# A 256-token trunk with a gated delta rule: the inverses' small transfers move from SyncE's queue to GpSimd's, and the scatter back is cut into four

## The chip, the cores and the metric

One core of a Trainium2 chip runs the whole kernel: a two-layer trunk for 256 tokens of width 2048, in float32. The metric is the device time of one execution in microseconds (us); lower is better. Every weight is read from HBM once per execution, 437 MB in all.

The engines are named as the profile names them: PE (TensorE's matmuls) and PEld (its weight loads), DVE (VectorE), ACT (ScalarE), POOL (GpSimd), and SP (SyncE). SP computes nothing here: it issues transfers in program order, and what stands behind a transfer that waits stands still too. SPq in a row of the profile is SP's queue.

## The reference, cut to what matters

The change lies in the first layer's mixer, a gated delta rule with 16 heads of width 128:

```python
kb = k * beta[..., None]
lower = jnp.where(strict, jnp.einsum('bnhid,bnhjd->bnhij', kb, k) * decay, 0.0)
rhs = jnp.concatenate([v * beta[..., None], kb * jnp.exp(g)[..., None]], axis=-1)
sol = lax.linalg.triangular_solve(lower, rhs, left_side=True, lower=True, unit_diagonal=True)
```

For every head a unit lower triangular system is solved, whose matrix comes from the products of the head's keys with each other. Nothing can be solved before the keys of that head exist, and no head's output can be had before its system is solved. Around it stand the projections k, q, z, v (`gdn_w_in`) and the output projection, and after it a feed-forward layer, an attention layer and a second feed-forward layer.

## The kernel before, in words

**The weight stream.** All projections go through `half` (L188): one piece of weights, 128 x 1024 float32 (512 KB), is loaded by SP into one of four `raw` tiles (L185), ACT rounds it to float32r (`hi`, L206), DVE forms the rest (`lo` = raw - hi, L207), and PE multiplies both by the 256 tokens (L228, L229: eight pairs of matmuls per piece). `raw`, `hi` and `lo` have four tiles each, so SP can load only some pieces ahead of PE. Each of z's and v's 16 heads takes two pieces.

**Things due later.** `after_halves(n, fn)` (L178) emits `fn` at the (n+1)th call of `half` from there on, just before that piece's load. In the order that SP executes, transfers therefore stand between two pieces of weights. SP's order is the written order; the other engines' orders come from a scheduler.

**The delta rule's inverses.** The order of the projections is k and q by heads, then z by heads, then v by heads.
- `products` (L552) makes a head's products of keys and writes them over the decays in `ma1` (first 128 tokens) and `ma2` (the other 128); DVE's L568 to L571 finish them. The sums of squares of keys and queries (`ssk`, `ssq`) come with them.
- `units_out` (L666) writes the 32 x 32 diagonal blocks of four heads to a DRAM scratch `um`: two tiles by four blocks, eight transfers (L675). It is emitted 11 pieces (`UM_LAG`) after each fourth head's products.
- `scales` (L506) writes the factors `cc`, transposed to `cT`, to the scratch `uc` with two transfers (L508), 11 pieces after the last products.
- `eliminate` (L677) is emitted two pieces later. It loads `um` and `uc` back with one block to a partition (L682, L684), and POOL inverts 128 blocks at once: L688, then 31 steps of a product (L692) and a subtraction (L695), then a transposing copy (L696). POOL also computes two inverse square roots (L174, L175) for `rq` and `rbt` around there.
- `there` (L698) writes the result to scratch in both layouts, `ut` and `un` (L699, L700), 31 pieces (`BACK_AT`) after the last products; `back` (L702), two pieces later, scatters it into the two tiles `T128` with 14 transfers (L707, L710).
- `merge` (L714), emitted at the 18th of the z and v projections, i.e. after all of z and the first of v, builds the 128-token inverses on PE from 32 x 32 matmuls (`iw`, L732; `ix`, L737) and 64 x 64 ones (`iy`).

All of these transfers are issued by SP, among the loads of weights.

Of the kernel before, what the change touches and what calls it, by code (L numbers as in the profile page):

```python
# [32 lines left out]
UM_LAG, BACK_AT, MERGE_AT = 11, 31, 17  # L33
# [21 lines left out]
class Lazy:  # L55
    """Tiles that are taken when they are first used."""
# [10 lines left out]
class Split:  # L67
    """A transposed activation [P, nk, 256] as two float32r parts, four k to a tile."""
# [22 lines left out]
class Trunk:  # L91
# [78 lines left out]
    def rsqrt(self, dst, src, scale):  # L170
        """dst = (src * scale + EPS) ** -0.5, exactly rounded powers, [P, n]."""
        nc = self.nc
        n = dst.free_size()
        nc.gpsimd.tensor_scalar(dst, src, scale, EPS, op0=ALU.mult, op1=ALU.add)  # L174
        nc.gpsimd.tensor_tensor(dst, dst, self.nhalf[:, :n], op=ALU.pow)  # L175

# [1 line left out]
    def after_halves(self, n, fn):  # L178
        """Emit fn once n more pieces of weights are under way."""
        self.due.append([n, fn])  # L180
# [7 lines left out]
    def half(self, src, name, apart=False):  # L188
        """One [P, 1024] piece of weights as two float32r parts that add up to it exactly."""
        nc = self.nc  # L190
        for d in self.due:
            d[0] -= 1
            if d[0] < 0:
                d[1]()
        self.due = [d for d in self.due if d[0] >= 0]
        cut = 2 if self.ahead else 1
        raw = self.ahead.pop(0) if self.ahead else self.raw(src, name)
        if apart:
            x = self.q(f"held_{name}", F32R)
            hi, lo = x[:, 0:1024], x[:, 1024:2048]  # L200
        else:
            hi = self.stp.tile([P, 1024], F32R, tag="hi", bufs=HI, name=f"hi_{name}")
            lo = self.stp.tile([P, 1024], F32R, tag="lo", bufs=LO, name=f"lo_{name}")
        for i in range(cut):
            c = slice(i * 1024 // cut, (i + 1) * 1024 // cut)
            nc.scalar.copy(hi[:, c], raw[:, c])  # L206
            nc.vector.tensor_tensor(lo[:, c], raw[:, c], hi[:, c].bitcast(F32), op=ALU.subtract)  # L207
        return hi, lo

    def wstat(self, srcs, xT, name, early=0):  # L210
        """For each source of weights, [P channels, 512]: columns 0:256 hold hi*hi, 256:512 the
        cross terms, for 256 tokens. Of the first `early` k the first 128 tokens go ahead."""
# [19 lines left out]
    def wstats(self, srcs, xT, first, name):  # L232
        """wstat over many sources, the first few side by side."""
# [5 lines left out]
    def add_halves(self, dst, ps, name, rows=slice(0, P), scaled=True):  # L239
        """The two halves' sum, for every token times its norm's factor."""  # L240
# [7 lines left out]
    def xstat(self, src, nk, xT, evac, name, ahead=0):  # L248
        """[tokens, 2048] = xT.T @ weights, a block of 512 columns at a time. In the last `ahead`
        pieces the first 128 tokens go ahead of the others."""  # L250
# [36 lines left out]
    def square(self, tt, q):  # L287
        """A part of the sum of h^2 over a token's row."""
        junk = self.t([P, 512], "jk", "junk", dtype=BF16)
        self.nc.scalar.activation(junk, self.h[:, tt, q * 512:(q + 1) * 512], AF.Square, accum_out=self.ssh[:, tt, q:q + 1])  # L290
# [8 lines left out]
    def pair(self, name):  # L299
        """Two banks, for even and odd k, so that two engines can read them at once."""  # L300
        return [self.ax(f"{name}_{i}") for i in range(2)]

    def enter_first(self):
        """What the first 128 tokens let begin: half of the first EARLY k of xT."""
# [19 lines left out]
    def enter(self):  # L324
        """xT = (h * weight).T in two parts, and every token's factor rsqrt(mean(h^2) + eps):
        self.r [tokens, 1] twice, self.rb the same along the columns of every partition."""
# [69 lines left out]
    def begin_post(self, which, name):  # L396
        """Room for a sublayer's result, and its norm's weights on every partition."""
# [24 lines left out]
    def update(self, tt, c, n):  # L422
        """h += result * factor, for n columns from c on."""
# [5 lines left out]
    def gdn(self):  # L429
# [12 lines left out]
        # the tensor engine's clock rises while it is kept busy  # L442
# [24 lines left out]
        # per token and head: c = beta / |k|^2, rb = beta / |k|, rq = scale / |q|  # L467
        g = {n: self.cst.tile([P, 2, NH], F32, name=n) for n in ("ssk", "ssq", "cc", "negc", "rbt", "rq")}
        dram = lambda n, shape: self.scr.tile(shape, F32, name=n)  # noqa: E731
# [4 lines left out]
        def multiply(h, kq):  # L474
            self.products(h, kq, MA1, MA2, g)
            if h % 4 == 3:
                self.after_halves(UM_LAG, lambda: self.units_out(h // 4, ma1, ma2))
# [28 lines left out]
        def scales():  # L506
            for p in range(2):
                nc.sync.dma_start(  # L508
# [3 lines left out]
        def eliminate():  # L512
            self.back = self.eliminate(cT, T128, units)
            fl = lambda x: x.rearrange("p a h -> p (a h)")  # noqa: E731
# [4 lines left out]

        self.after_halves(UM_LAG, scales)  # L520
        self.after_halves(UM_LAG + 2, eliminate)
        self.after_halves(BACK_AT, lambda: self.back[0]())
        self.after_halves(BACK_AT + 2, lambda: self.back[1]())
# [28 lines left out]
    def products(self, h, kq, MA1, MA2, g):  # L552
        """The masked and decayed products of a head's keys with its keys and queries."""
# [30 lines left out]
    def gates_and_decays(self, ps, ma1, ma2, szt):  # L584
# [3 lines left out]
        # room of z's tiles: after[s, j] = s > j, upto[s, i] = s <= i, and what is needed on the way  # L588
# [27 lines left out]
        # log1p(e) = e * ln(1 + e) / ((1 + e) - 1), and e where 1 + e rounds to 1  # L616
# [16 lines left out]
        # decay[j, i] = exp(sum of g over j < s <= i)  # L633
        sfx = self.t([P, NH], "sfx", "sfx", bufs=1)
        for q in range(4):
# [15 lines left out]
            v = lambda x: x.rearrange("p (h i) -> p h i", h=4)  # noqa: E731  # L651
# [12 lines left out]
    # The inverses of I + c M: on blocks of 32 tokens by elimination with one block to a partition,  # L664
    # unit = (p, b, h), then block by block on the tensor engine.
    def units_out(self, grp, ma1, ma2):  # L666
        """Four heads' diagonal blocks to their units' rows."""
        for p, ms in ((0, ma1), (1, ma2)):
# [3 lines left out]
            for b in range(4):  # L672
                bs = slice(b * 32, (b + 1) * 32)
                u = (p * 4 + b) * NH + grp * 4
                self.nc.sync.dma_start(self.um[u:u + 4].rearrange("h j i -> j h i"), m[bs, h0:h0 + 4, 0, bs])  # L675

    def eliminate(self, cT, T128, room):  # L677
# [4 lines left out]
        nc.sync.dma_start(m, um)  # L682
        cu = self.t([P, 32], "uc", "uc", bufs=1)
        nc.sync.dma_start(cu, uc)  # L684
# [13 lines left out]
        def there():  # L698
            nc.sync.dma_start(ut, m)  # L699
            nc.sync.dma_start(un, tu)  # L700

        def back():  # L702
            for p in range(2):
                for b in range(4):
                    u = slice((p * 4 + b) * NH, (p * 4 + b + 1) * NH)
# [6 lines left out]
        return there, back  # L712

    def merge(self, ma1, ma2, cc, T128, room):  # L714
        """T128[p][c, h, i]: the transposed inverses on 128 tokens. Its blocks' inverses as they
        are lie in [0:64, :, 64:128] and [64:96, :, 0:32] until they have been used."""
# [41 lines left out]
    def head(self, h, vT, MA1, MA2, T128, negc, rb, rq):  # L758
# [15 lines left out]
        # the heads' outputs, tokens on partitions  # L774
# [85 lines left out]
    def weights_of(self, h, kq, aT):  # L860
        """aT[key, (q0 k0 | q1 k0 | q1 k1)]: the transposed difference of the two softmaxes."""
# [155 lines left out]
```

## Time and profile before

| | |
|---|---|
| time, median of 3 runs | 2448.48 us (2447.5 to 2450.08) |
| profiled execution: its own time, the span from first to last instruction | 2455.4 us |
| PE busy | 2421.8 us, 99% |
| PEld busy | 2070.3 us, 84% |
| DVE busy | 1666.7 us, 68% |
| ACT busy | 1197.6 us, 49% |
| POOL busy | 116.7 us, 5% |
| mean granted TensorE clock | 0.993 of full speed |

The profiled execution is one run with the hardware profiler on; nothing of its time is given beside the span. Shares are means over the whole span. The stage in question, the first mixer with its output projection, takes about the first 510 us; z's and v's projections and the delta rule stand in it from about 230 us on.

A row of a timeline gives the start in us from the beginning of the span, the duration, engine, line, operation, out<-in, and a count where several were merged; in brackets stands how long the engine was idle before it, and who ended that.

### The profile page before, as it was taken

What the parts mean: (1) busy time and instruction counts of PE and PEld (TensorE: products, weight loads), DVE (VectorE), ACT (ScalarE), POOL (GpSimd) and SP (SyncE); (2) the same over time, 40 slices, a digit from 0 to 9 for tenths busy, and PEclk for the clock granted to TensorE, in tenths of its full rate; (3) what the DMA queues carried; (4) which work ended last, traced back from release to release, by engine and by line L of the source; (5) the groups of instructions that cost most, each with busy time, mean ns of one, the idle gap of its engine ahead of it and who ended that gap; (6) DMA issues with size and microseconds to landing.
All of it is one profiled execution on the core that took longest, in us unless ns stands there. A gap on an engine that the chain in (4) does not pass through costs nothing.

```text
span 2455.4 us, 35164 instructions
## 1 busy us (share of the span) xinstructions
PE 2421.8 (99%) x13267; PEld 2070.3 (84%) x13267; DVE 1666.7 (68%) x2603; ACT 1197.6 (49%) x1958; POOL 116.7 (5%) x185
## 2 busy tenths in 40 slices
PE   9999979999999999999999999999999999999998
PEld 7788869878888888888888888888888888888887
DVE  6888647857777777764446677555877777774444
ACT  6755424546444444443446555444644444444442
POOL 0100730100000000000000000000000000000000
PEclk9999989999999999999999999999999999999999
DMA  6365543444555555565554554555555555556554
GB/s 224 105 200 167 194 141 121 163 163 162 190 188 187 185 187 188 184 206 194 194 192 146 198 183 162 170 189 189 169 192 189 189 189 190 192 189 210 191 196 153
DMA packets 134731, 443.21 MB, mean 181 GB/s; under 512 B 26144, under 2 KB 26400, under 8 KB 134048
## 3 DMA queue, kind: packets, MB, share of 16 engines
q1 hardware_dynamic: 134560, 440.95, 54.4%
q8 instruction: 104, 1.70, 0.3%
q14 instruction: 67, 0.55, 0.1%
HBM read 437.21 MB, written 3.69 MB: 180 GB/s over the span
## 4 chain that ended last, share of the span: by engine, by line
PE 93%; POOL 2%; DVE 1%; ACT 1%; DMA 1%; SPq 1%; issue 1%; DVEq 0%; POOLq 0%; ACTq 0%
PE ps_up L228 26%; PE ps_up L229 13%; PE ps_d L283 7%; PE ps_d L284 7%; PE ps_d L282 6%; PE ps_v L228 3%; PE ps_ak L228 2%; PE ps_aq L228 2%; PE ps_k L228 2%; PE ps_q L228 2%; PE ps_v L229 1%; PE ps_wo L283 1%; PE ps_av L282 1%; PE ps_av L284 1%; PE ps_av L283 1%; PE ps_ao L284 1%
## 5 line engine op out<-in xcount | busy, mean ns | idle before, releaser
L228 PE MATMUL ps_up<-xT_f,hi_up 128*128 128x512 f32 x2752 | 964.1, 396 | 0.0
L229 PE MATMUL ps_up<-xT_f,lo_up 128*128 128x256 f32 x2752 | 767.5, 279 | 1.6 <-DVE lo_up L207 1.6
L228 PEld LDWEIGHTS ps_up<-xT_f,hi_up 128*128 128x128 f32 x2752 | 516.4, 188 | 123.6
L206 ACT CAST hi_up<-raw_up 128x1024 fp32r<-128x1024 f32 x344 | 361.1, 1051 | 482.1 <-issue 328.9
L207 DVE TENSOR_TENSOR lo_up<-raw_up,hi_up 128x1024 fp32r<-128x1024 f32 x344 | 421.1, 1225 | 202.4 <-ACT hi_up L206 202.1
L229 PEld LDWEIGHTS ps_up<-xT_f,lo_up 128*128 128x128 f32 x2752 | 518.3, 188 | 3.0 <-DVE lo_up L207 2.7
L207 DVE TENSOR_TENSOR lo_d<-raw_d,hi_d 128x1024 fp32r<-128x1024 f32 x168 | 205.8, 1225 | 224.2 <-ACT hi_d L206 224.2
L206 ACT CAST hi_d<-raw_d 128x1024 fp32r<-128x1024 f32 x168 | 177.1, 1054 | 256.5 <-PE ps_d L284 239.6
L282 PE MATMUL ps_d<-hi_d,hT 128*128 128x512 f32 x672 | 261.5, 389 | 0.0
L284 PE MATMUL ps_d<-hi_d,hT 128*128 128x512 f32 x672 | 261.4, 389 | 0.0
L283 PE MATMUL ps_d<-lo_d,hT 128*128 128x512 f32 x672 | 261.4, 389 | 0.0
L282 PEld LDWEIGHTS ps_d<-hi_d,hT 128*128 128x128 f32 x672 | 126.2, 188 | 26.2
L284 PEld LDWEIGHTS ps_d<-hi_d,hT 128*128 128x128 f32 x672 | 126.2, 188 | 26.2
L283 PEld LDWEIGHTS ps_d<-lo_d,hT 128*128 128x128 f32 x672 | 126.2, 188 | 26.1
L228 PE MATMUL ps_z<-xT_in,hi_z 128*128 128x512 f32 x256 | 92.4, 404 | 9.8 <-ACT hi_z L206 9.8
L228 PE MATMUL ps_v<-xT_in,hi_v 128*128 128x512 f32 x256 | 97.8, 417 | 2.3 <-ACT hi_v L206 2.3
L228 PE MATMUL ps_k<-xT_in,hi_k 128*128 128x512 f32 x240 | 88.3, 406 | 0.8 <-DVE s L244 0.8
L228 PE MATMUL ps_ak<-xT_kv,hi_ak 128*128 128x512 f32 x240 | 86.9, 402 | 0.0
L813 DVE SCALAR_TENSOR_TENSOR gy<-gs,c_fconv,gy 128x255 f32<-128x255 f32 (+1 forms) x176 | 84.5, 480 | 2.8
L228 PE MATMUL ps_q<-xT_in,hi_q 128*128 128x512 f32 x240 | 85.5, 397 | 0.3 <-DVE s L244 0.3
L228 PE MATMUL ps_aq<-xT_q,hi_aq 128*128 128x512 f32 x224 | 78.2, 392 | 0.0
L174 POOL TENSOR_SCALAR qr<-q 128x1 f32<-128x1 f32 x8 | 1.5, 193 | 1588.0 <-DVE q L409 1588.0
(382 smaller groups left out, 4122.9 us busy)
## 6 DMA issues: line engine op xcount, KB each, us to landing
raw_up<-in_w_up SPq DMA_DIRECT2D x344, 512.0 KB, 4.2
raw_d<-in_w_dn SPq DMA_DIRECT2D x176, 512.0 KB, 3.5
raw_z<-in_w_in SPq DMA_DIRECT2D x32, 512.0 KB, 3.6
raw_v<-in_w_in SPq DMA_DIRECT2D x32, 512.0 KB, 3.5
raw_wo<-in_w_out SPq DMA_DIRECT2D x32, 512.0 KB, 4.1
raw_av<-in_w_v SPq DMA_DIRECT2D x32, 512.0 KB, 3.4
raw_ao<-in_w_o SPq DMA_DIRECT2D x32, 512.0 KB, 3.5
raw_k<-in_w_in SPq DMA_DIRECT2D x30, 512.0 KB, 3.5
```

What stands on the lines that cost most here:

```text
L174: nc.gpsimd.tensor_scalar(dst, src, scale, EPS, op0=ALU.mult, op1=ALU.add)
L206: nc.scalar.copy(hi[:, c], raw[:, c])
L207: nc.vector.tensor_tensor(lo[:, c], raw[:, c], hi[:, c].bitcast(F32), op=ALU.subtract)
L228: nc.tensor.matmul(to, hi[:, w], x, start=(k == 0 and tt != 1), stop=False)
L229: nc.tensor.matmul(lt, lo[:, w], lx, start=False, stop=(k == KD - 1))
L282: nc.tensor.matmul(ps, xh, hi[:, w], start=(k == 0), stop=False)
L283: nc.tensor.matmul(ps, xh, lo[:, w], start=False, stop=False)
L284: nc.tensor.matmul(ps, xl, hi[:, w], start=False, stop=(k == nk - 1))
L813: nc.vector.scalar_tensor_tensor(y[:, j:S], s[:, 0:S - j], w[:, l, f, 2 - j:3 - j], y[:, j:S], op0=ALU.mult, op1=ALU.add)
```

## The change

The lines of the changed kernel have the same numbers up to L697 and numbers higher by one from the scatter on (L708 for L707, L733 for L732); comments that fell away are left out of the diff.

```diff
-UM_LAG, BACK_AT, MERGE_AT = 11, 31, 17
+BACK_AT, MERGE_AT = 30, 17
...
         def multiply(h, kq):
             self.products(h, kq, MA1, MA2, g)
             if h % 4 == 3:
-                self.after_halves(UM_LAG, lambda: self.units_out(h // 4, ma1, ma2))
+                self.units_out(h // 4, ma1, ma2)
...
         def scales():
             for p in range(2):
-                nc.sync.dma_start(
+                nc.gpsimd.dma_start(
                     self.uc[p * 64:(p + 1) * 64].rearrange("(b h) i -> h b i", b=4),
                     cT[p * NH:(p + 1) * NH].rearrange("h (b i) -> h b i", b=4))
...
-        self.after_halves(UM_LAG, scales)
-        self.after_halves(UM_LAG + 2, eliminate)
-        self.after_halves(BACK_AT, lambda: self.back[0]())
-        self.after_halves(BACK_AT + 2, lambda: self.back[1]())
+        scales()
+        eliminate()
+        for i in range(4):
+            self.after_halves(BACK_AT + i, lambda i=i: self.back(i))
...
-                self.nc.sync.dma_start(self.um[u:u + 4].rearrange("h j i -> j h i"), m[bs, h0:h0 + 4, 0, bs])
+                self.nc.gpsimd.dma_start(self.um[u:u + 4].rearrange("h j i -> j h i"), m[bs, h0:h0 + 4, 0, bs])
...
-        nc.sync.dma_start(m, um)
+        nc.gpsimd.dma_start(m, um)
         cu = self.t([P, 32], "uc", "uc", bufs=1)
-        nc.sync.dma_start(cu, uc)
+        nc.gpsimd.dma_start(cu, uc)
...
-        def there():
-            nc.sync.dma_start(ut, m)
-            nc.sync.dma_start(un, tu)
-
-        def back():
+        nc.gpsimd.dma_start(ut, m)
+        nc.gpsimd.dma_start(un, tu)
+
+        def back(i):
             for p in range(2):
                 for b in range(4):
+                    if b != i:
+                        continue
...
-        return there, back
+        return back
```

The 38 transfers of `um`, `uc`, `units`, `ut` and `un` are now issued by POOL, at the place in the program where their data are made; the 14 of the scatter stay with SP, in four parts (one for each block of 32 tokens: four, four, four and two transfers) ahead of four pieces in a row, from one piece earlier than `there` stood.

The first place is POOL's order where the last four heads' blocks go out and the elimination begins (`ma` tiles hold the products, `um_d` and `uc_d` are the scratch, `units` the elimination's tile). Before:

```order
L687 MEMSET units 128x32
L174 TENSOR_SCALAR rq<-ssq 128x32
L175 TENSOR_TENSOR rq<-rq,nhalf 128x32
L174 TENSOR_SCALAR rbt<-ssk 128x32
L518 TENSOR_SCALAR rq<-rq 128x32
L175 TENSOR_TENSOR rbt<-rbt,nhalf 128x32
L516 TENSOR_TENSOR rbt<-rbt,bgT 128x32
L688 TENSOR_TENSOR units<-units,uc 128x1024
```

And with the change, the last heads' transfers alone:

```order
L675 DMA um_d<-ma_3_388 32x4x32 x4
L174 TENSOR_SCALAR rq<-ssq 128x32
L175 TENSOR_TENSOR rq<-rq,nhalf 128x32
L174 TENSOR_SCALAR rbt<-ssk 128x32
L675 DMA um_d<-ma_1_390 32x4x32 x4
L518 TENSOR_SCALAR rq<-rq 128x32
L175 TENSOR_TENSOR rbt<-rbt,nhalf 128x32
L508 DMA uc_d<-cT 16x4x32 x2
L682 DMA units<-um_d 128x1024
L516 TENSOR_TENSOR rbt<-rbt,bgT 128x32
L684 DMA uc<-uc_d 128x32
L688 TENSOR_TENSOR units<-units,uc 128x1024
```

Ahead of and among the same six small operations now stand twelve transfers, eight of them behind the first power (L175), and L688 comes last.

The second place is SP's order around the scatter. Before (`t_0` and `t_1` are the two `T128` tiles):

```order
L185 DMA raw_z_0_1_3403<-in_w_in 128x1024
L185 DMA raw_z_0_0_3432<-in_w_in 128x1024
L699 DMA ut_d<-units 128x1024
L700 DMA un_d<-units 128x1024
L185 DMA raw_z_0_1_3456<-in_w_in 128x1024
L185 DMA raw_v_0_0_3485<-in_w_in 128x1024
L707 DMA t_0_2541<-ut_d 32x16x32
```

With the change:

```order
L185 DMA raw_z_0_1_3405<-in_w_in 128x1024
L708 DMA t_0_2549<-ut_d 32x16x32
L711 DMA t_0_2549<-un_d 32x16x32
L708 DMA t_1_2550<-ut_d 32x16x32
L711 DMA t_1_2550<-un_d 32x16x32
L185 DMA raw_z_0_0_3438<-in_w_in 128x1024
L708 DMA t_0_2549<-ut_d 32x16x32
L711 DMA t_0_2549<-un_d 32x16x32
L708 DMA t_1_2550<-ut_d 32x16x32
L711 DMA t_1_2550<-un_d 32x16x32
L185 DMA raw_z_0_1_3464<-in_w_in 128x1024
```

The first transfer that needs the elimination now stands ahead of both pieces of z's last head, where before it stood between them, and it is a read of `ut`, where before it was the write of `ut`. On PE the first 16 of `merge`'s `iw` matmuls now stand ahead of z's last head, where before the first `iw` stood between the two pieces of v's first head.

## Rows read from the trace of the kernel before

**Rows 1.** The page's first part: span, and busy time by engine.

```profile
span 2455.4 us, 35164 instructions
PE 2421.8 (99%) x13267; PEld 2070.3 (84%) x13267; DVE 1666.7 (68%) x2603; ACT 1197.6 (49%) x1958; POOL 116.7 (5%) x185
```

**Rows 2.** PE's timeline around z's last head and v's first.

```profile
334.99 0.80 PE L228 MATMUL ps_z<-xT_in,hi_z 128*128 128x512 f32 x1 [9.80 <-ACT hi_z L206]
...
340.56 0.40 PE L228 MATMUL ps_v<-xT_in,hi_v 128*128 128x512 f32 x1
...
343.43 0.62 PE L732 MATMUL iw<-t,ma 32*32 32x32 f32 x14
346.36 0.51 PE L228 MATMUL ps_v<-xT_in,hi_v 128*128 128x512 f32 x1 [2.31 <-ACT hi_v L206]
...
352.68 1.54 PE L732 MATMUL iw<-t,ma 32*32 32x32 f32 x36
354.15 0.50 PE L228 MATMUL ps_v<-xT_in,hi_v 128*128 128x512 f32 x1
```

**Rows 3.** Stretches of 2 us: length, busy by engine (PE, PEld, DVE, ACT, POOL), granted clock, DMA.

```profile
332.00:334.00 2.00, 0.00 (x0) 0.00 (x0) 0.00 (x0) 0.11 (x1) 0.00 (x0) 0.50 0.88 314
...
350.00:352.00 2.00, 2.00 (x8) 1.71 (x8) 1.71 (x2) 0.80 (x1) 0.00 (x0) 0.50 0.77 227
```

**Rows 4.** Waits of SP's queue, 300 to 360 us: total, times, longest.

```profile
SPq L699 <- POOL units L696: 21.4, 1, 21.4
```

**Rows 5.** The chain of waits, 318 to 362 us: start, us, what.

```profile
327.42 4.13 DMA un_d<-units
...
331.93 0.49 SPq L707
332.46 0.49 SPq L710
...
341.23 4.01 DMA raw_v<-in_w_in
```

**Rows 6.** POOL's timeline, from the decays' last operation to the elimination's end.

```profile
99.03 0.15 POOL L687 MEMSET units<- 128x32 f32 x1
253.28 0.68 POOL L174 TENSOR_SCALAR rq<-ssq 128x32 f32<-128x32 f32 x1 [154.10 <-ACT jq L564]
254.04 5.45 POOL L175 TENSOR_TENSOR rq<-rq,nhalf 128x32 f32<-128x32 f32 x1
...
265.78 0.96 POOL L516 TENSOR_TENSOR rbt<-rbt,bgT 128x32 f32<-128x32 f32 x1
268.22 2.40 POOL L688 TENSOR_TENSOR units<-units,uc 128x1024 f32<-128x1024 f32 x1 [1.49 <-DMA uc<-uc_d]
270.70 0.30 POOL L692 TENSOR_TENSOR pr<-units 128x31 f32<-128x31 f32 x1
271.08 1.14 POOL L695 TENSOR_TENSOR units<-units,pr 128x31 f32<-128x31 f32 x1
...
325.11 1.91 POOL L696 COPY units<-units 128x1024 f32<-128x1024 f32 x1
```

**Rows 7.** POOL in two stretches with the same 16 shapes: length, busy, clock, DMA.

```profile
270.70:285.56 14.86, 13.64 (x16) 1.00 0.72 246
317.30:325.04 7.74, 6.56 (x16) 1.00 0.00 0
```

**Rows 8.** DVE's timeline: the last heads' products, and its last operation before the idle stretch.

```profile
248.53 0.42 DVE L569 TENSOR_TENSOR ma<-p,ma 128x256 f32<-128x256 f32 x1
...
317.66 0.43 DVE L246 TENSOR_TENSOR zs<-zs,rb_in 128x256 f32<-128x256 f32 x1
```

**Rows 9.** DMA issues: out<-in, queue, count, KB each, median us to landing.

```profile
um_d<-ma SPq DMA_DIRECT2D x32, 16.0 KB, 2.0
units<-um_d SPq DMA_DIRECT2D x1, 512.0 KB, 5.8
ut_d<-units SPq DMA_DIRECT2D x1, 512.0 KB, 2.6
```

**Rows 10.** z's weights (raw_z), 290 to 345 us: seven loads.

```profile
DMA to landing us min/median/max: 3.4/3.4/5.9
```

## The prediction

> **What bounds the kernel now.** The page comes first: of a span of 2455.4 us PE is busy 2421.8 us [rows 1]. The stream of weights through PE is the bound; a change counts only where it makes or closes a hole in PE, or where PE runs slower. PE's timeline shows the holes that belong to this change [rows 2]. Ahead of the second piece of z's last head PE is idle for 9.80 us (until 334.99), ahead of the second piece of v's first head for 2.31 us. The short stretches show what follows a hole [rows 3]: the granted clock is 0.50, the lower of the two levels (1.2 GHz), in the idle stretch around 333 us and again at 350 to 352 us, where PE is busy. So the piece that starts at 334.99 lasts until 340.56, 5.57 us, while the next, at full clock, takes 2.87 (340.56 to 343.43) [rows 2].
>
> The hole's cause is found in SP's waits: it stood 21.4 us at L699 until POOL's copy L696 was done [rows 4], and every load of weights behind stood with it. Then the two results are written (the second lands 4.13 us after its issue), the scatter goes out at 0.53 us a transfer (331.93 to 332.46), and only at 341.23 the next load [rows 5]. So the start of POOL's elimination and its length decide. POOL idles 154.10 us until the last query's sum of squares, runs the small operations from 253.28 to 266.74, waits 1.49 us for data and starts L688 at 268.22; the copy ends at 327.02 [rows 6].
>
> One property of the elimination matters below. Its shapes run up from 31 to 256 columns and down again, so its first 16 and last 16 operations are the same work: 14.86 us while DVE works, 7.74 us in the last stretch [rows 7], nearly all of it after DVE's last operation at 317.66 [rows 8]. Beside a working DVE it is 1.92 times slower.
>
> **The change, part by part.** I compare when PE starts the third piece of v (354.15 before [rows 2]); all holes of the change lie ahead of it, and behind it the work is the same.
>
> *Early transfers.* The first three groups of four heads (24 transfers) move to POOL's idle 154 us and off SP's queue, where PE had no hole: nothing gained. If that cover were gone, they would delay the elimination by their issue time.
>
> *Price of an issue on POOL, d.* No row of before shows a transfer issued by POOL. Nearest below: SP's 0.49 us for a scatter transfer [rows 5]. Nearest above: 2.0 us, as if POOL stood until `um` has landed [rows 9]. A reason excludes a gain: on POOL the issues stand in series with the elimination. I take SP's 0.49 plus the 0.84 by which POOL's same-sized operations differ beside a busy DVE (1.14 against 0.30 [rows 6]): d = 1.33.
>
> *The start.* The fourth group's first four transfers are ready at 248.95 [rows 8] and end at 248.95 + 4d = 254.27, 0.99 later than 253.28, where the power chain began. From its start to the start of its last operation (253.28 to 265.78 [rows 6]) are 12.5 us, and four more `um`, two `uc_d` and the `units` load now stand in between: 7d = 9.31. So the load is issued by 276.1. It landed 5.8 us after its issue began [rows 9], 5.5 after it ended: L688 starts at about 281.5, not 268.22, **13.3 us later**. The `uc` load, issued 0.96 + d later and small, I let land with it.
>
> *The elimination.* What slides by 13.3 us was run beside DVE and now falls after 317.66, where DVE has nothing to do because its weights are held up: 13.3 / 1.92 = 6.9. It ends at 327.02 + 6.9 = 333.9.
>
> *The way back.* POOL issues both writes (2d = 2.7), and SP's first scatter transfer waits for the landing, by 2.3 (2.6 less SP's issue [rows 9]) to 3.7 (4.13 less it [rows 5]): 3.0. SP is free at 339.6; before, its waits were over at 331.6. Queued behind it are both pieces of z's last head.
>
> *Restart.* Four scatter transfers at 0.53 (2.12), then the load: 4.01 [rows 5] to 5.9 [rows 10], I take 5.0; ACT's cast to PE's start 1.12 (345.24 to 346.36, [rows 2, 5]). That is 8.24. One piece at the low clock 5.57, three at 2.87, and the second half of the tile's `iw` (32 of 64 records at 1.54 / 36 each, 1.4) [rows 2]; the first half hides in the hole. Together 23.8, and the scatter (some 2.7 us a piece on SP) keeps ahead of PE. The 2.31 us hole and the second slow stretch of before are gone in this sum: that is the gain of the four parts. PE starts v's third piece at 339.6 + 23.8 = 363.4, not 354.15: **+9.3 us**.
>
> Bounds: d = 0.49 with the fast landings starts L688 6.4 us later and gives +2.3; d = 0 gives about nothing. d = 2.0 with slow landings starts it 20.6 later and gives +16.
>
> The profiled execution took 2455.4 us, 0.3% above the median of 2448.48; I put the sum on the median unscaled: 2457.8.
>
> On the lock between POOL and DVE: the row shows 14.86 against 7.74 us. The Trainium skill (SBUF — State Buffer, "SBUF: two separate sides") says that a DVE operation with two SBUF inputs and a POOL operation that reads SBUF shut each other out for whole instructions, and that a transfer issued by POOL can't write its descriptors while DVE holds the ports in its two-port modes. This speaks against the change; by it each issue could wait out one of DVE's operations, and the sum would come to about +12 (an estimate from that page's rule, with 1.2 us for such a DVE operation).
>
> **The rivals.**
>
> *1. Cheap issue: no change.* POOL only hands a transfer over, d below 0.65. L688 then starts 3 to 8 us later and the sum lies between 0 and +4.9, 2451 at its middle. For it: SP's bare issue is 0.49. Against it: POOL does its own operations between and slows beside DVE, which SP does not. The Trainium skill (DMA: Bandwidth & Descriptors, "Anatomy of one DMA") calls descriptor generation small and puts most of a POOL transfer's fixed time after the issue; no row here shows it.
>
> *2. The elimination meets DVE less: faster.* Which operations collide depends on when they start. If from 281.5 on none did, the middle part would take 46.6 / 1.92 = 24.3 us (270.70 to 317.30 before [rows 6, 7]) and the rest 7.74; with L688, the copy and the gaps it ends at 318.0, SP is free at 323.7, and v's third piece starts at 347.5: -6.6, so 2441.8. It decides once SP is free before 330.3, that is, once the elimination ends by 324.6. Against it: DVE runs the same operations at the same pace as long as weights flow, so the collisions should be as many.
>
> *3. POOL stands longer than a landing, d above 2.* Beyond 1.33 each 0.1 us of d costs about 0.8 us (seven and four issues through the 1.92, and two on the way back), so d = 2.5 gives +18: 2466.5. For it: eight issues stand in a row on the critical engine.
>
> That the transfers do not leave earlier where it matters is part of the forecast: the fourth group left SP as soon as DVE was done, and now half of it stands behind a power of 5.45 us [rows 6].
>
> **How the numbers follow.** Forecast (d from 0.65 to 2, +5 to +16): 0.65. Rival 1: 0.19. Rival 2: 0.06. Rival 3: 0.10. A measurement of this kernel can tell about 0.2% (4.9 us) from no change. So faster 0.06, same 0.19, slower 0.65 + 0.10 = 0.75. The range reaches down into rival 1, to +1 (2449.5), and up past the upper bound into rival 3, +18.5 (2467); the likeliest case alone is 2453.5 to 2464.5.
>
> **What would show it.** POOL's L688 starts near 281 us (275 if d is small); the copy L696 ends near 334; SP's longest wait is at its first scatter transfer (L708) and lasts over 30 us; PE's hole ahead of z's last head runs from about 322 us, one piece (2.87) earlier than before, to about 348, some 25 us; the 2.31 us hole in v's first head is gone. I am wrong if L688 starts before 272 us, if the elimination is shorter than 46 us, or if PE's hole there stays under 13 us.

## The result, and the profile after

| | before | after |
|---|---|---|
| median | 2448.8 us (7 runs, 2445.61 to 2456.68) | 2459.58 us (7 runs, 2452.94 to 2467.58) |
| ratio, 95% interval | 1 | 1.0051 [1.0036, 1.0065] |
| profiled execution, span | 2455.4 us | 2464.6 us |
| z's first matmul | 235.90 us | 234.91 us |
| L688 starts / the copy L696 ends | 268.22 / 327.02 | 275.00 / 328.94 |
| v's third piece starts | 354.15 us | 357.20 us |
| w_out's first matmul starts / its last ends | 477.04 / 577.17 | 481.45 / 586.07 |

The changed kernel is slower, by about 12 us going by the ratio and by 9.2 us going by the two spans. A second series (e9) gave 1.0038 [1.0022, 1.0054]. Single times of one kernel lie up to 20 us apart, mostly because each of the two stages with `w_up` runs at one of two paces in an execution, whatever the kernel (last section). Both profiles above have the same paces there, and their distance is 8.9 us at w_out's end and 9.2 us at the end of the span. The ratio says 12 because three of the seven times of after and one of before have a stage more at the slower pace; runs at the same pace lie 9 to 10 us apart.

The page's first part of the kernel after, to compare with [rows 1]:

```profile
span 2464.6 us, 35217 instructions
PE 2423.4 (98%) x13267; PEld 2070.4 (84%) x13267; DVE 1667.0 (68%) x2603; ACT 1198.0 (49%) x1958; POOL 132.5 (5%) x223
```

POOL has 38 records more, the transfers, and is busy 15.8 us longer. Its timeline around the elimination, to compare with [rows 6] (a row of three points marks rows that are left out):

```profile
247.91 2.20 POOL L675 DMA_DIRECT2D um_d<-ma  x4 [42.25 <-DVE ma L568]
...
253.05 5.47 POOL L175 TENSOR_TENSOR rq<-rq,nhalf 128x32 f32<-128x32 f32 x1
...
258.88 2.27 POOL L675 DMA_DIRECT2D um_d<-ma  x4
...
261.70 5.45 POOL L175 TENSOR_TENSOR rbt<-rbt,nhalf 128x32 f32<-128x32 f32 x1
267.12 1.10 POOL L508 DMA_DIRECT2D uc_d<-cT  x2
268.22 0.58 POOL L682 DMA_DIRECT2D units<-um_d  x1
...
271.58 0.60 POOL L684 DMA_DIRECT2D uc<-uc_d  x1 [1.53 <-DMA uc_d<-cT]
275.00 2.86 POOL L688 TENSOR_TENSOR units<-units,uc 128x1024 f32<-128x1024 f32 x1 [2.81 <-DMA uc<-uc_d]
...
327.04 1.90 POOL L696 COPY units<-units 128x1024 f32<-128x1024 f32 x1
328.89 0.60 POOL L699 DMA_DIRECT2D un_d<-units  x1
```

An issue takes POOL 0.55 to 0.60 us, for 16 KB as for 512 KB. The eight that stand behind the first power are 4.6 us, and the round trip of `uc` adds two waits, 1.53 and 2.81 us, where before there was one of 1.49 [rows 6]. The DMA issues, with the median from issue to landing in the last column:

```profile
um_d<-ma POOLq DMA_DIRECT2D x32, 16.0 KB, 2.4
units<-um_d POOLq DMA_DIRECT2D x1, 512.0 KB, 5.2
...
uc_d<-cT POOLq DMA_DIRECT2D x2, 8.0 KB, 3.4
uc<-uc_d POOLq DMA_DIRECT2D x1, 16.0 KB, 3.3
```

SP's wait, and its queue where the wait ends (before: [rows 4, 5]):

```profile
SPq L708 <- DMA ut_d<-units: 31.8, 1, 31.8
```

```profile
333.64 0.33 SPq L708 DMA_DIRECT2D t<-ut_d  x1
...
335.67 0.43 SPq L185 DMA_DIRECT2D raw_z<-in_w_in  x1
```

PE around the hole (before: [rows 2]):

```profile
336.61 1.88 PE L733 MATMUL iw<-t,ma 32*32 32x32 f32 x32 [15.23 <-DMA t<-un_d]
...
341.13 0.79 PE L228 MATMUL ps_z<-xT_in,hi_z 128*128 128x512 f32 x1 [2.64 <-ACT hi_z L206]
...
357.20 0.50 PE L228 MATMUL ps_v<-xT_in,hi_v 128*128 128x512 f32 x1
```

The hole is longer (15.23 and 2.64 us for 9.80 and 2.31), yet v's third piece starts only 3.05 us later. The other part of the 9 us comes later, and most visibly in w_out. There PE waits for ACT, whose order the scheduler has written in another way. ACT before, and after:

```profile
505.71 0.40 ACT L796 CAST oT_gdn<-of 128x256 fp32r<-128x256 f32 x1 [1.72 <-DVE of L795]
506.02 1.04 ACT L206 CAST hi_wo<-raw_wo 128x1024 fp32r<-128x1024 f32 x1
507.24 0.41 ACT L796 CAST oT_gdn<-of 128x256 fp32r<-128x256 f32 x1 [0.18 <-DVE of L795]
```

```profile
512.74 0.40 ACT L797 CAST oT_gdn<-of 128x256 fp32r<-128x256 f32 x1 [2.89 <-DVE of L796]
513.37 0.41 ACT L797 CAST oT_gdn<-of 128x256 fp32r<-128x256 f32 x1 [0.22 <-DVE of L796]
513.68 3.88 ACT L206 CAST hi_wo<-raw_wo 128x1024 fp32r<-128x1024 f32 x4
```

Before, a cast of weights stands between the last two heads' outputs. After, it stands behind both, four casts run in a row, and PE has nothing until the first is done. PE's own order is not what differs here: the last four heads' outputs stand behind the same six and seven pieces of w_out before and after.

```profile
514.77 0.73 PE L282 MATMUL ps_wo<-hi_wo,oT_gdn 128*128 128x512 f32 x2 [1.96 <-ACT hi_wo L206]
```

### The profile page after: what moved, and what is told of

Same layout as the page of the kernel before. It is cut to its first block, busy times and chain, and to the rows that moved or that the text cites. A ratio compares the mean times of both kernels' runs of the same rounds, so it can differ in the third digit from the quotient of the medians.

```text
span 2464.6 us, 35217 instructions
## 1 busy us (share of the span) xinstructions
PE 2423.4 (98%) x13267; PEld 2070.4 (84%) x13267; DVE 1667.0 (68%) x2603; ACT 1198.0 (49%) x1958; POOL 132.5 (5%) x223
## 4 chain that ended last, share of the span: by engine, by line
PE 93%; POOL 2%; DVE 2%; ACT 1%; DMA 1%; issue 1%; SPq 0%; DVEq 0%; POOLq 0%; ACTq 0%
PE ps_up L228 26%; PE ps_up L229 13%; PE ps_d L282 6%; PE ps_d L284 6%; PE ps_d L283 6%; PE ps_v L228 3%; PE ps_ak L228 2%; PE ps_aq L228 2%; PE ps_k L228 2%; PE ps_q L228 2%; PE ps_v L229 1%; PE ps_av L282 1%; PE ps_av L284 1%; PE ps_av L283 1%; PE ps_ao L284 1%; PE ps_ao L283 1%
```

## The experiments

The expectations weigh accounts of the loss against each other: by theory 1 all of it arises at the hole, by theory 2 a part arises behind it, from the orders that the scheduler wrote, and by theory 3 (in e7) one chain sets the end whatever PE does. One way of counting serves all experiments. From stretches of 1 us I add up PE's idle time (length less busy time) and its loss at the low clock (busy time times one less the granted clock), apart for 310 to 360 us (the hole), 360 us to w_out's first matmul (merge and heads) and w_out. "x" is the end of the copy counted from z's first matmul; "place" is the number of pieces after which SP first waits for the elimination. Times in us.

| kernel | place | x | hole: idle, clock | heads: clock | w_out: idle, clock | w_out ends | ratio to before | same pace |
|---|---|---|---|---|---|---|---|---|
| before | 31 | 91.1 | 12.6, 5.6 | 3.4 | 2.2, 0.0 | 577.2 | 1 | 0 |
| after | 30 | 94.0 | 18.5, 2.8 | 5.1 | 4.1, 1.7 | 586.1 | 1.0051 [1.0036, 1.0065] | +9 to +10 |
| after, again (e9) | 30 | 95.0 | 20.7, 3.9 | 0.0 | 4.0, 1.6 | 582.3 | 1.0038 [1.0022, 1.0054] | +9.5 |
| powers emitted late (e3) | 30 | 95.1 | 19.4, 3.5 | 5.1 | 4.1, 0.0 | 585.8 | 1.0026 [1.0009, 1.0042] | +8 |
| way in on SP (e1) | 30 | 91.8 | 16.3, 3.2 | 1.7 | 1.5, 1.7 | 577.2 | 0.9983 [0.9964, 1.0003] | -2 |
| way out as before (e2) | 31 | 96.5 | 16.0, 4.0 | 5.1 | 3.2, 1.6 | 582.1 | 1.0002 [0.9988, 1.0017] | +4 to +5 |
| before, merge later (e4) | 31 | 92.7 | 14.4, 5.7 | 6.8 | 1.9, 0.0 | 581.8 | 0.9997 [0.9982, 1.0011] | +1 to +2 |
| powers behind (e5) | 30 | 89.1 | 14.0, 3.8 | 1.7 | 1.5, 0.0 | 573.8 | 0.9977 [0.9968, 0.9987] | -3.8 |
| heads' scaling on ACT (e6) | 30 | 94.4 | 18.6, 4.1 | 6.8 | 3.2, 3.1 | 588.0 | 1.0029 [1.0019, 1.0039] | +8.2 |
| scatter and merge later (e7) | 32 | 96.3 | 14.5, 2.8 | 1.7 | 1.5, 0.0 | 574.1 | 0.9998 [0.9989, 1.0006] | -0.1 |
| e5, e6 and e7 together (e8) | 32 | 91.2 | 11.3, 3.0 | 5.1 | 2.7, 0.0 | 574.7 | 0.9991 [0.9982, 1.0000] | -2.2 |
| scatter in one place, late (e10) | 33 | 97.8 | 14.6, 8.4 | 0.0 | 1.5, 0.0 | 573.3 | 0.9995 [0.9979, 1.0011] | -1.8 |
| e5 and e10 together (e11) | 33 | 92.1 | 13.1, 3.5 | 5.9 | 3.2, 1.6 | 579.1 | 1.0019 [1.0002, 1.0037] | +2.7 |
| e5, scatter one piece later (e12) | 31 | 90.0 | 11.3, 6.0 | 3.5 | 1.5, 0.0 | 574.7 | 0.9974 [0.9957, 0.9991] | -4.7 |

A row's trace is one execution and its ratio a series, so a single trace's w_out end can be some us off what the series shows: after and its repeat end w_out at 586.1 and 582.3, and before has one trace only.

The last column is the difference from before in mean time, in us, between runs at the same pace. A run's span times its mean granted clock leaves out what the low clock costs; these products lie in groups some 9 us apart, one group for each stage at the slower pace, and the profiled runs lie in the groups that their traces show. The intervals are 0.7 to 1.5 us to either side; two values stand where some runs of before lie between two groups, or are few. The ratio mixes the paces: in e2's series 3 of 12 runs have both stages at the slower pace, in that of before beside it 22 to 25 of 35.

**The way in alone undone (e1).** The same edit as for `um` is made for `uc` and the two loads, and `scales` and `eliminate` are delayed as before.

```diff
-                self.units_out(h // 4, ma1, ma2)
+                self.after_halves(UM_LAG, lambda: self.units_out(h // 4, ma1, ma2))
...
-                self.nc.gpsimd.dma_start(self.um[u:u + 4].rearrange("h j i -> j h i"), m[bs, h0:h0 + 4, 0, bs])
+                self.nc.sync.dma_start(self.um[u:u + 4].rearrange("h j i -> j h i"), m[bs, h0:h0 + 4, 0, bs])
```

> The changed kernel with only the way in undone: um, uc and the two loads go back to SyncE's queue with their old delay; the two writes stay on GpSimd and the scatter stays in four parts. Theory 1 (all of the loss comes from the elimination: it starts 6.8 us and ends 1.9 us later, and the scatter then holds z's last head): L688 starts at 268 again, the copy ends at 327.0, the restart comes some 2 us earlier, so about 2457.5 against 2459.6 of the changed kernel; w_out's stretch from its first to its last matmul stays at about 97 us. Theory 2 (more than half of the loss arises behind the hole, because the written order of PE now has the merge and the heads about one piece of v later and the last heads come late for w_out): in this kernel's order the first head stands behind 6.5 pieces of v (8.4 in the changed kernel, 7.3 before), so w_out's stretch goes back to 93 us or less and the time is about 2453.

L688 started at 266.79, the copy ended at 325.51, the hole's restart was 3.5 us earlier than after, and w_out ended 8.8 us earlier. PE's idle time at the hole is 2.2 us less, at w_out 2.6 less, and the low clock took 3 us less. Both theories' effects are there; the ratio is 1 within its interval, and at the same pace this version is 2 us faster than before.

**The way out alone undone (e2).**

```diff
-BACK_AT, MERGE_AT = 30, 17
+BACK_AT, MERGE_AT = 31, 17
...
-        for i in range(4):
-            self.after_halves(BACK_AT + i, lambda i=i: self.back(i))
+        self.after_halves(BACK_AT, lambda: self.back[0]())
+        self.after_halves(BACK_AT + 2, lambda: self.back[1]())
...
-        nc.gpsimd.dma_start(ut, m)
-        nc.gpsimd.dma_start(un, tu)
+        def there():
+            nc.sync.dma_start(ut, m)
+            nc.sync.dma_start(un, tu)
```

> The changed kernel with only the way out undone: the way in stays on GpSimd at once, but ut and un are written by SyncE and the scatter stands in one block two pieces behind, as before. The elimination should start at 275 and its copy end at about 329, as in the changed kernel. Theory 1: the hole is the one of before plus 1.9 us: about 2451. Theory 2 adds nothing, since the first head stands behind 7.4 pieces of v (7.3 before): about 2451 too, w_out's stretch 93 us. If the way in itself carried the loss (a slow transfer that holds up the weights), it would be about 2459.

L688 started at 275.60, as after, and the copy ended at 330.63, 1.7 us later than after. The ratio is 1, but that is the paces' doing: at the same pace e2 is 4 to 5 us slower than before, and its w_out ended 4.9 us later. So the way in alone on GpSimd costs about half of the loss, the way out alone nothing, and both together 9 to 10 us: the halves do not simply add.

**The powers emitted later (e3).** The two inverse square roots and what goes with them are emitted with the scatter instead of with the elimination.

```diff
         def eliminate():
             self.back = self.eliminate(cT, T128, units)
-            fl = lambda x: x.rearrange("p a h -> p (a h)")
...
+        self.after_halves(BACK_AT, powers)
```

> The changed kernel with the two powers and their small operations emitted behind the elimination, so that no 5.45 us operation stands between the transfers' data and their issue. PE's written order is that of the changed kernel (first head behind 8.44 pieces of v). The elimination should start at about 267 instead of 275. Theory 1: it ends 4 to 6 us earlier (half of the 8 is lost beside VectorE), and the hole is shorter by as much: about 2454.5, with v's third piece at about 352.5. Theory 2: the same 4 to 6 us at v's third piece, but w_out's stretch stays at 97 us, so the kernel stays some 4 us slower than before although v's third piece starts earlier than the 354.15 of before: about 2454. If the start of the elimination did not matter: 2459.6.

The edit did not do what it was meant to do. POOL's timeline of this run has the powers where they were:

```profile
252.86 5.47 POOL L175 TENSOR_TENSOR rq<-rq,nhalf 128x32 f32<-128x32 f32 x1
...
261.51 5.46 POOL L175 TENSOR_TENSOR rbt<-rbt,nhalf 128x32 f32<-128x32 f32 x1
```

The scheduler orders POOL by its own account, and the place of emission did not bind it. The run counts as a repeat of the changed kernel, and is some 8 us slower than before, like it.

**The merge later in the kernel before (e4).**

```diff
-UM_LAG, BACK_AT, MERGE_AT = 11, 31, 17
+UM_LAG, BACK_AT, MERGE_AT = 11, 31, 18
...
-                vT = self.t([P, S], f"vT{h}", "vT", bufs=3)
+                vT = self.t([P, S], f"vT{h}", "vT", bufs=4)
```

> The kernel before with the merge (and with it the heads) emitted one projection later (MERGE_AT 18, one more vT tile); transfers, elimination, scatter and the hole stay as before. In PE's written order the first head stands behind 9.4 pieces of v instead of 7.3, and head 14 behind 1.9 blocks of w_out instead of 1.5. Theory 1: no hole changes, 2448.8. Theory 2: the last heads come late for w_out, whose stretch grows from 93 to 97 us or more: 2453 to 2456.

w_out did not wait longer (1.9 us idle for 2.2), and the time moved by 1 to 2 us where theory 2 asked for 4 to 7. A later place of the heads alone is not what costs; theory 2 in that form fell.

**The powers really behind (e5).** The elimination's POOL instructions, and the powers behind them, are held in the written order.

```diff
-            self.back = self.eliminate(cT, T128, units)
+            with self.tc.manual_schedule(engines={mybir.EngineType.Pool}):
+                self.back = self.eliminate(cT, T128, units)
+                ...
```

> The changed kernel with GpSimd's order held as written around the elimination, so that the two powers (5.45 us each) really stand behind it and not between the transfers (in the run that only emitted them later the scheduler put them back to the front). um's last four transfers can then go at about 253.6, uc_d at 258.8, and with the landings of the changed kernel's trace (3.4 and 3.3 us after the issue) L688 starts at about 266 to 267 instead of 275. Theory 1 (place of the elimination): the copy ends at about 325 instead of 328.9 and w_out's last matmul lies 3 to 4 us ahead of the changed kernel's. Theory 2 (place plus written order): in this kernel's order the first head stands behind 6.5 pieces of v again, as in the run with the way in on SyncE, so both shares go and w_out ends where it ended before, 8 to 9 us ahead of the changed kernel. Rival (the transfers on GpSimd are what costs): nothing gained, w_out ends with the changed kernel's.

```profile
253.98 0.56 POOL L676 DMA_DIRECT2D um_d<-ma  x1 [3.59 <-DVE ma L572]
...
259.51 1.06 POOL L508 DMA_DIRECT2D uc_d<-cT  x2 [2.97 <-DVE cT L504]
260.87 0.58 POOL L683 DMA_DIRECT2D units<-um_d  x1 [0.29 <-issue]
263.44 0.56 POOL L685 DMA_DIRECT2D uc<-uc_d  x1 [2.00 <-DMA uc_d<-cT]
...
266.84 2.82 POOL L689 TENSOR_TENSOR units<-units,uc 128x1024 f32<-128x1024 f32 x1 [1.65 <-DMA uc<-uc_d]
```

Now the transfers do leave when their data exist, the elimination starts at 266.84, the copy ends at 324.37, and PE's first stop at the hole is 10.63 us instead of 15.23:

```profile
331.22 1.88 PE L734 MATMUL iw<-t,ma 32*32 32x32 f32 x32 [10.63 <-DMA t<-un_d]
```

w_out ended 12.3 us ahead of the changed kernel's, and this version is faster than the kernel before, by 0.2%. Transfers on GpSimd as such are thus not what costs; at the hole, what stood between them was. The gain over before is not at the hole, though, where PE is idle 1.4 us longer than before: the traces show it in the low clock (5.5 us for 9.0) and at w_out (1.5 us idle for 2.2), so no run shows that moving the transfers gained it. PE's and ACT's written orders changed with it (a cast of weights stands between the last heads' outputs again), so the hole's share (4.5 us of idle time) and the tail's (2.6) are not told apart by this run alone.

**The heads' scaling on ACT (e6).**

```diff
-            nc.vector.tensor_scalar(vs[:, p, :], c[p], rb[:, p, h:h + 1], None, op0=ALU.mult)
+            nc.scalar.activation(vs[:, p, :], c[p], AF.Copy, scale=rb[:, p, h:h + 1])
```

> The changed kernel with one operation of every head (values times rbt, twice 128x128) on ScalarE instead of VectorE. Up to the first head's start PE's written order and the hole are those of the changed kernel (first head behind 8.44 pieces of v in both), the last heads stand one piece earlier (head 12 behind 31.2 pieces of v instead of all 32). Theory 1 (all loss in the hole): w_out's stretch stays at 104 us, its last matmul where it is in the changed kernel. Theory 2 (half the loss at the tail, where the last heads come late for w_out): PE's idle time between 490 and 530 us falls from 4.1 us to 2 or 2.5 and w_out ends 3 to 4 us earlier, with the restart at the hole unchanged.

The hole stayed (18.6 us), as both said. The wait of 1.96 us at w_out stayed too; PE's idle time there was 3.2 instead of 4.1, and w_out ended 1.9 us later instead of 3 to 4 earlier. The run does not test theory 2 as it was meant to: in PE's order the first twelve heads stand about a piece of weights earlier than in the changed kernel, but the last four stand where they stood, behind six and seven pieces of w_out.

**Scatter and merge later (e7).**

```diff
-BACK_AT, MERGE_AT = 30, 17
+BACK_AT, MERGE_AT = 32, 18
...
```

> The changed kernel with scatter and merge both two pieces later (BACK_AT 32, MERGE_AT 18, one more vT tile). The elimination is the changed kernel's; SyncE can load two pieces more before it stands still. Theory 1: PE's hole shrinks by two pieces, 5 to 6 us, and the time by as much. Theory 3 (the chain of elimination, merge, heads and w_out sets the end, and idle time only moves along it): the hole shrinks by 5 to 6 us, but the first head stands behind 10.4 pieces of v, PE waits as much more at w_out, and w_out's last matmul comes within 2 us of the changed kernel's.

The hole's idle time fell by 4.0 us, although the copy ended 2.3 us later, and w_out did not wait longer but shorter. Theory 3 (a chain that sets the end whatever PE does) fell. The ratio fell from 1.004 or 1.005 to 0.9998: two pieces of place, with the heads' order that came with them, gave back the whole loss.

**Three together (e8).** Edits of e5, e6 and e7.

> Three things together on the changed kernel: powers behind the elimination, scatter and merge two pieces later, one operation of every head on ScalarE. If the shares add (place of the elimination 3 to 4 us, hole 5 to 6, tail 1 to 3), w_out ends 3 to 5 us ahead of the kernel before: a ratio of about 0.998. If the chain sets the end (theory 3), the two pieces give nothing and it ends with the kernel before, ratio 1.000.

The hole was the shortest, with e12's (11.3 us), but the clock in the heads' stretch and w_out's wait (1.33 us, for the last head's output itself) gave part of it back. No better than e5.

**The changed kernel again (e9).**

> The changed kernel itself once more, for a second trace and so that its time stands beside the next three on one chip. Both theories: 1.003 to 1.005 of the kernel before; PE idle some 18 us around the hole and 4 us at w_out's start; w_out ends some 9 us behind the kernel before.

Slower than before, as said; hole and tail came again (20.7 and 4.0 us). The loss at the low clock in the heads' stretch did not: 0.0 for 5.1 us. Stretches of 20 us, after and again (length, busy by engine, granted clock, DMA share, GB/s):

```profile
360.00:380.00 20.00, 20.00 (x326) 18.12 (x325) 13.52 (x21) 4.66 (x7) 0.52 (x1) 0.81 0.41 142
```

```profile
360.00:380.00 20.00, 20.00 (x346) 18.18 (x345) 16.80 (x26) 5.50 (x10) 0.52 (x1) 1.00 0.47 159
```

**The scatter in one place, late (e10), with the powers behind (e11), and one piece later (e12).**

```diff
-            self.after_halves(BACK_AT + i, lambda i=i: self.back(i))
+            self.after_halves((33, 33, 33, 33)[i], lambda i=i: self.back(i))
```

In e12 the four numbers are 31, 32, 33 and 33; e11 and e12 have the edit of e5 too.

> The changed kernel with only the place of the scatter changed: its four parts stand together ahead of the 34th piece instead of ahead of the 31st to 34th; powers, elimination, writes on GpSimd and merge as in the changed kernel. Theory 1 in its present form (PE's idle time at the hole = end of the elimination, less 2.87 us for every piece that SyncE may still load before its first wait for the scatter's data): three pieces later gives 8.6 us less idle time, against which the block of 14 transfers ahead of one load brings back a hole like the 2.3 us of before; so some 12 us of idle time around the hole instead of 18.5, and w_out ends about 6 us ahead of the changed kernel (3 us behind the kernel before). If the spread itself, and not the place, is what matters, the hole stays at 18 us.

> Powers behind the elimination (as in the fastest run so far) and the scatter in one place ahead of the 34th piece. Theory 1: 14.0 us of idle time at the hole become 5.4 plus a hole of about 2.3 for the block: w_out ends 9 to 10 us ahead of the kernel before, ratio 0.995 to 0.996. Rival (the tail takes it back, as with the scatter and the merge two pieces later together with the other two edits): 0.998 to 0.999, with more idle time at w_out's start and more slow clock in the merge.

> Powers behind the elimination, and the four parts ahead of the 32nd, 33rd and (the last two) 34th piece: one piece later than in the run with the powers behind, with the same written order of PE (first head behind 6.5 pieces of v). Theory 1: 2.9 us less idle time at the hole, 11.1 instead of 14.0, w_out ends 6 us ahead of the kernel before, ratio about 0.9965. Rival: as the run before it, 0.9977.

e10 recovered what was lost: 14.6 us of idle time at the hole (12 expected), ratio 0.9995. e11 was a miss, 1.0019 where 0.995 to 0.996 was expected: its first hole was short, as reckoned, but behind it came another of 9.12 us.

```profile
332.99 0.66 PE L734 MATMUL iw<-t,ma 32*32 32x32 f32 x16 [3.96 <-DMA t<-un_d]
...
342.76 0.79 PE L228 MATMUL ps_v<-xT_in,hi_v 128*128 128x512 f32 x1 [9.12 <-ACT hi_v L206]
```

SP issued the 14 transfers from 329.65 on and the next load of weights only at 337.82:

```profile
337.82 11.99 SPq L185 DMA_DIRECT2D raw_v<-in_w_in  x8
```

So the spread in four is worth something where the elimination ends early: the block then is the hole. e12, with the spread kept and one piece later, had the 11.3 us of idle time that were reckoned (11.1), and is faster than before like e5; its w_out ended at 574.7, not earlier than e5's, because the low clock took 4.0 us more.

**What the runs give together.** In the six kernels with place 30, the idle time at the hole is x less 74.3 to 75.8, 75.3 in the mean. Less 2.87 us for every piece of later place, the same sum gives 13.0 for before (12.6 measured), 14.6 for e4 (14.4), 11.9 for e12 (11.3), 15.3 and 10.1 for e7 and e8 (14.5, 11.3) and 13.9 for e10 (14.6). Two miss: e2 by 2.3 (18.3, measured 16.0), because the second hole of 2.31 us in v's first head, which before and e4 have behind the same block of scatter transfers, is not there (PE has 32 `iw` matmuls ahead of it), and e11 by 4.9 (8.2, 13.1), for the block. After against before is thus 2.9 us for the later end of the copy and 2.87 for the place, which makes 5.8 of the 5.9 us between 12.6 and 18.5.

The second part is the tail. The wait of 1.96 us for `hi_wo` is in the six kernels (after, e2, e3, e6, e9, e11) where ACT casts the last two outputs with no weights between them, with 3.2 to 4.1 us of idle time at w_out, and in none of the other eight, with 1.5 to 2.7. That it goes with ACT's order is shown by the rows; that order alone was not turned round in an experiment. Still open is the clock in the heads' stretch, 0.0 to 6.8 us: it differs between two executions of one kernel, and no run isolates it.

## Why the prediction was right or wrong

The time came out where it was put, 2459.58 for 2457.8, and 9 to 10 us at the same pace for +9.3, but by a sum whose main term was too large and which lacked another. That these two errors nearly cancel is luck.

- **Price of an issue, d: wrong.** 0.55 to 0.60 us measured, 1.33 taken. It was rival 1's value. Adding the 0.84 us by which POOL's own operations lengthen beside DVE had no ground in a row: four issues beside DVE's work took 2.20 and 2.27 us. The rule of the Trainium skill on locked-out descriptor writes (SBUF — State Buffer, "SBUF: two separate sides") speaks of DVE's two-port modes; no row here shows DVE in one, so these issues neither bear it out nor refute it, and the +12 that was worked out from it did not come. What the Trainium skill says of a small price for descriptors (DMA: Bandwidth & Descriptors, "Anatomy of one DMA") agrees with the 0.55 to 0.60 us.
- **The start: right in kind, half in size.** L688 went from 268.22 to 275.00, 6.8 us for 13.3. I let `uc` land with `units`; it landed last, since its second transfer could only be issued when the first had landed, 3.4 us after its issue on POOL for 1.4 on SP. The start lies where rival 1 put it (3 to 8 us later).
- **The elimination: gained more than reckoned.** 53.9 us from L688's start to the copy's end, 58.8 before. Of the slide of 6.8 us only 1.9 was left, where the factor of 1.92 would have left 3.5. DVE's steady work ended earlier too, since the weights stopped a piece earlier: its last `lo_z` ahead of the hole began at 311.12 for 314.93, and the elimination's end ran beside two pairs of small operations. In e7 and e10, which start L688 at 273.91 and 273.40 and let the weights flow two and three pieces longer, the elimination took 56.5 and 57.8 us. Before, and after:

```profile
314.93 1.23 DVE L207 TENSOR_TENSOR lo_z<-raw_z,hi_z 128x1024 fp32r<-128x1024 f32 x1 [0.36 <-ACT hi_z L206]
```

```profile
311.12 1.22 DVE L207 TENSOR_TENSOR lo_z<-raw_z,hi_z 128x1024 fp32r<-128x1024 f32 x1 [1.21 <-ACT hi_z L206]
...
321.87 0.42 DVE L244 TENSOR_TENSOR zs<-ps_z,c_z 128x256 f32<-128x256 f32 x1 [4.44 <-ACT c_z L243]
```

- **The way back and the restart: right.** From the copy's end to the first scatter transfer 4.7 us (5.7 reckoned), from there to PE's start 7.5 (8.24), from PE's start to v's third piece 16.1 (15.6). The place one piece earlier, the hole from 321 us on, the single long wait of SP at L708 (31.8 us) and the end of the 2.31 us hole came as said. That it is the four parts that end this hole is not shown: e2, with one block, does not have it either. Half of the idle time that the hole adds is the place: 2.87 of 5.9 us.
- **+9.3 us at v's third piece: wrong**, +3.05, or +4.0 counted from z's first matmul; in the second trace +4.2, or +6.0.
- **"Behind it the work is the same": wrong, and the step that failed.** PE, DVE and ACT have as many instructions as before; the orders that the scheduler wrote are not the same. Of the 8.9 us at w_out's end in the first trace 3.1 lie at the hole, 1.9 are idle time in w_out, which goes with ACT's order there, 1.7 are low clock in w_out and 1.7 low clock in the heads' stretch. The low clock can't be put down to that order: e1 has 1.7 us in w_out without it, e3 none with it, and the heads' share is missing in the second trace. What causes this part stays open.
- **Rivals.** Up to v's third piece rival 1 is what happened: its price, its start, and its 0 to +4.9 us there (+6.0 in the second trace, counted from z's first matmul, lies above). It too held the work behind to be the same, so its 2451 lies below both series. The forecast came nearer to the time by an error of 5 to 6 us at the hole that the tail and the clock made up for. Rival 2 (faster) needed the elimination to meet DVE less; it did, the elimination being 4.9 us shorter, but its start was 6.8 us later. 3 is out, d being 0.6.
- **Early transfers gain nothing: right**, as far as the trace shows: z's first matmul came 1.0 us earlier, but in the other kernels it came 0.6 to 2.5 us earlier too, those with the way in on SP among them.

## What to carry to other kernels

Work that is handed to another queue "as soon as its data exist" leaves only when everything ahead of it on that engine is done: look at what the engine's order puts between the data and the issue (here two powers of 5.45 us) and at round trips that now stand in series. Where a load queue waits for a computation, every piece of place in that queue costs PE one piece, so put the first wait as late as its users allow, and spread the block only if the data are there in time. Where a scheduler orders the engines, an edit also changes orders far behind it; compare these orders at the next stage's start, and hold an order explicitly if it matters, since a later place in the code did not hold it.

## What the runs showed of the hardware that was not expected

- **An issue on GpSimd costs little more than one on SP**, 0.55 to 0.60 us for 16 KB and for 512 KB, where SP's rows show 0.33 to 0.49; eight beside DVE's tensor operations were no longer (2.20 and 2.27 us for four). The small writes to the scratch land later, 3.4 us for 1.4 (`uc_d`) and 2.4 for 2.0 (`um`), but the 16 KB load `uc` landed sooner, 3.3 for 5.7.
- **The same matmuls at full clock run at one of two paces in a stage.** Between 700 and 900 us, in `w_up` of the first feed-forward layer, the granted clock is 1.00 and PE is never idle in both of these profiles: before, and with the way in on SP (out<-in, shapes, count, busy us, mean ns):

```profile
L228 PE MATMUL ps_up<-xT_f,hi_up 128*128 128x512 f32 x567 | 200.4, 399 | 0.0
```

```profile
L228 PE MATMUL ps_up<-xT_f,hi_up 128*128 128x512 f32 x578 | 200.4, 394 | 0.0
```

That is 2% over the stage, some 9 us for each of the two layers. All 14 traces have 394 or 399 ns in either layer, nothing between, and from w_out's end to the end of the span they take 1869 to 1871 us with no layer at the slower pace (seven traces), 1878 to 1880 with one (five) and 1887 to 1888 with both (two). The pace changes from one execution to another of the same kernel: e1's twelve times lie at 2447 to 2448, at 2455 and at 2465 to 2467 us. What sets it is open; it is why stages were compared here by w_out's end, which lies ahead of it, and times between runs at the same pace.
